# Neighbourhood attention's first keys and queries: other places in the pool, and loads ahead of the fill's third W block

## The chip, the core and the metric

The kernel runs on one core of a Trainium2 chip. The metric is the device time of one execution in microseconds, as the median of the runs. PE is TensorE (matmuls; PEld its weight loads), ACT is ScalarE, DVE is VectorE, POOL is GpSimd, and SP is SyncE, which here does nothing but issue DMAs. L72 is line 72 of the kernel.

## What is computed

One layer of an encoder on 1024 tokens of width 1024 in float32: a half-step SwiGLU, a mixing layer, a half-step SwiGLU. The mixing layer projects its input to queries, keys and values of a retention and of a 2-D neighbourhood attention and to gates, runs both, and merges them. The change is at the start of the neighbourhood attention:

```python
u = rms_norm(x, mix_pre_norm)
ret_q, ret_k, ret_v, ret_g, na_q, na_k, na_v, gate_ret, gate_na = split(u @ w_mix_in)
# neighbourhood attention: 8 heads of 64, tokens on a 16 x 64 grid
for each row r and block of 16 query columns:
    k, v = 8 rows x 32 columns around the block
    s = (q / 8) @ k.T + rel_bias, masked to 8 x 16 around each query
    o = softmax(s) @ v
```

## The kernel before

**Arithmetic.** Float32 products are made of reduced ones: `split` (L55 to L65) makes of a tile a high part on ACT (L61, or L64 with a scale) and a low part on DVE (L62, L65), and `mm3` (L85 to L90) sums three matmuls, high by high, high by low and low by high.

**W blocks.** `load_w` takes a 512 KB block of weights from DRAM with one DMA on SP (L72) into a tile `wraw` (4 buffers) and splits it in two pieces `wh`, `wl` (8 buffers each).

**The work before.** The projections for attention and gates run as `Pairs`, with operands a11, a12, a22 and the sums s1 to s4, high and low parts of 8 KB in a partition each. In the last of these jobs PE reads them in the order s2, a12, s3, s1, a22, s4. The pool that holds s1 to s4 is then closed, and its bytes are given to the pools `mix` and `na`.

**Neighbourhood attention** is `na_cores`. It runs over 4 pairs of heads, and for each pair over 8 units (`NA_UNITS`: which bias, which half of the rows, which column block). `load(hp)` takes the pair's keys (`kraw`, L879) and splits them into `k0` and `k1`; `qload(hp)` takes its queries in four DMAs (L867) into two tiles `qraw`; `qsplit` makes the operands `qh`, `ql` of one column block. `scores` (L909 the matmuls, L910 to L918 the softmax), `flip` (L928, transposes) and `values` are the three stages, run one unit behind each other. `load(hp + 1)` comes in unit 4 of a pair and `qload(hp + 1)` in unit 5; `qraw` has two buffers and a pair uses both, so the next pair's queries wait until `qsplit` has read the old ones for the last time (unit 4). The tile `ot` takes a pair's output, which POOL stores (L978).

**The fill.** PE's time between these stages is filled with other matmuls: `fill` is a generator `products()`, which yields after each `mm3`. Its first part is `vproj` for retention's values: 2 halves of the columns, each in groups of 3, 3 and 2 token tiles, each over 8 k-tiles, with one W block for two k-tiles. `fill(12)` is called ahead of unit 0, then 2 + 2 steps in each unit. So the third W block of the first group (k = 4) is asked for at step 12, of the second at step 36 (unit 6), and in the second half of the columns at steps 76 (unit 16) and 100 (unit 22).

**What sets the order.** The kernel names tiles; a scheduler turns the program into one fixed list for each engine. It takes instructions by their place in the program, but one whose operands or bytes aren't free yet lets later ones pass. Each engine and the SP queue then work their list strictly in order. A tile gets its bytes by the order in which a pool's tags are first asked for, and with `reuse_waits="tile"` its first use waits for the last use of just those earlier tiles that lay there. Before, the order in `na` is kraw, k0, k1, qraw, the q operands, bt, s, the v tiles, pth, ptl, ot, from byte 77152 of a partition on. Retention's pool `ret` later begins at the same byte.

After the fill's steps have run past retention's values, `ret_cores` follows; its first v tiles (L1069) lie at byte 101728.

## Time and profile before

| | |
|---|---|
| median of 3 runs | 2270.53 us (2268.02 to 2271.82) |
| the profiled execution | 2266.95 us |
| its span, first to last instruction | 2265.2 us |
| granted PE clock, mean over the span | 0.992 |
| PE busy | 2204.2 us |
| DMA | 439.91 MB, 194 GB/s |

Times in the profile are microseconds from the span's start. A row of a timeline gives start, length, engine, line, operation, what it writes and reads, how many were merged, and in brackets the engine's idle time before it with what ended it. A row SPq is a DMA's issue, not its transfer. A row of waits gives who waited for whom, the sum, how often, and the longest. Matmuls overlap: a row's 0.39 us is its own length, and the next one starts 0.23 us later. Of PE's idle time nothing comes back by itself: the span ends when PE's list ends.

### The profile page before, as it was taken

Reading aid. Unit: us, or ns where it says so; the run is one execution under the profiler, and the core shown is the slowest. Engines: PE = TensorE matmul, PEld = TensorE weight load, DVE = VectorE, ACT = ScalarE, POOL = GpSimd, SP = SyncE. Lnnn points to the kernel's source line nnn. Section 1 sums busy time; section 2 is a strip of 40 time slices with the busy share of each in tenths; the row PEclk is TensorE's granted clock in tenths of the full one; section 3 lists DMA queues with packets and bytes.
Section 4 is the critical chain, followed back from the end, with each engine's and each line's share of the span. In section 5 each row is a group of like instructions: output and inputs, shape, how many; then the busy total and the mean of one; then the engine's idle time right before and its main releaser. Section 6 shows DMA issues by size and latency. Waiting matters only on the chain. (4 is left out here: it accounts for less than half of the span.)

```text
span 2265.2 us, 30039 instructions
## 1 busy us (share of the span) xinstructions
PE 2204.2 (97%) x10232; PEld 1830.1 (81%) x10232; DVE 1641.4 (72%) x2928; ACT 984.5 (43%) x2054; POOL 575.8 (25%) x747
## 2 busy tenths in 40 slices
PE   6899999999998999999999999999999999999998
PEld 5688888888786887878888888887778888888886
DVE  7898878765558757769885678544998787876444
ACT  5444434332344322248885676323644343433232
POOL 1121212168521122311101222101112121215942
PEclk9999999999999999999999999999999999999999
DMA  6354434597545554557655466764345444449765
GB/s 251 134 181 150 177 130 170 187 387 294 199 174 174 180 173 134 145 181 241 217 173 174 151 230 233 259 232 144 117 156 188 149 161 147 154 157 378 283 225 180
DMA packets 150345, 439.91 MB, mean 194 GB/s; under 512 B 19056, under 2 KB 46832, under 8 KB 148080
## 3 DMA queue, kind: packets, MB, share of 16 engines
q1 hardware_dynamic: 108912, 305.84, 39.4%
q0 software_dynamic: 41280, 132.15, 16.2%
q8 instruction: 81, 1.33, 0.2%
q14 instruction: 72, 0.59, 0.1%
HBM read 297.41 MB, written 144.70 MB: 195 GB/s over the span
## 5 line engine op out<-in xcount | busy, mean ns | idle before, releaser
L62 DVE TENSOR_TENSOR wl<-wraw,wh 128x512 fp32r<-128x512 f32 x472 | 317.1, 689 | 66.3 <-ACT wh L61 66.0
L61 ACT CAST wh<-wraw 128x512 fp32r<-128x512 f32 x476 | 274.2, 618 | 169.2 <-PE ps L89 69.2
L88 PE MATMUL ps<-wh,g 128*128 128x512 f32 x484 | 188.8, 390 | 0.0
L89 PE MATMUL ps<-wl,g 128*128 128x512 f32 x484 | 188.7, 390 | 0.0
L90 PE MATMUL ps<-wh,g 128*128 128x512 f32 x484 | 188.5, 390 | 0.0
L552 ACT ACTIVATE c<-c 128x512 f32<-128x512 f32 x88 | 55.5, 632 | 208.0 <-DVE c L517 107.6
L62 DVE TENSOR_TENSOR wl<-w,wh 128x512 fp32r<-128x512 f32 x77 | 77.9, 1031 | 86.3 <-ACT wh L61 86.1
L62 DVE TENSOR_TENSOR wl<-x,wh 128x512 fp32r<-128x512 f32 x77 | 78.4, 1035 | 78.3 <-ACT wh L61 77.1
L61 ACT CAST wh<-t 128x512 fp32r<-128x512 f32 x58 | 36.0, 621 | 195.0 <-DVE t L511 194.9
L88 PE MATMUL ps<-a11h,wh 128*128 128x512 f32 x276 | 111.5, 404 | 7.9 <-ACT wh L61 7.9
L90 PE MATMUL ps<-a11h,wl 128*128 128x512 f32 x276 | 109.7, 398 | 7.3 <-DVE wl L62 7.2
L90 PE MATMUL ps<-a12h,wl 128*128 128x512 f32 x276 | 108.7, 394 | 3.4 <-DVE wl L62 3.4
L88 PE MATMUL ps<-a12h,wh 128*128 128x512 f32 x276 | 109.7, 397 | 0.5 <-ACT wh L61 0.3
L89 PE MATMUL ps<-a11l,wh 128*128 128x512 f32 x276 | 109.8, 398 | 0.1
L90 PE MATMUL ps<-a22h,wl 128*128 128x512 f32 x280 | 109.3, 390 | 0.6 <-DVE wl L62 0.6
L88 PE MATMUL ps<-a22h,wh 128*128 128x512 f32 x280 | 109.8, 392 | 0.0
L89 PE MATMUL ps<-a22l,wh 128*128 128x512 f32 x280 | 109.2, 390 | 0.0
L89 PE MATMUL ps<-a12l,wh 128*128 128x512 f32 x276 | 108.2, 392 | 0.0
L89 PEld LDWEIGHTS ps<-wl,g 128*128 128x128 f32 x484 | 90.9, 188 | 19.1 <-DVE wl L62 0.5
L90 PEld LDWEIGHTS ps<-wh,g 128*128 128x128 f32 x484 | 90.9, 188 | 18.8
L88 PEld LDWEIGHTS ps<-wh,g 128*128 128x128 f32 x484 | 90.9, 188 | 18.7
L88 PE MATMUL ps<-s2h,wh 128*128 128x512 f32 x232 | 91.9, 396 | 6.6 <-ACT wh L61 6.5
(438 smaller groups left out, 6411.4 us busy)
## 6 DMA issues: line engine op xcount, KB each, us to landing
wraw<-in_dram SPq DMA_DIRECT2D x202, 512.0 KB, 4.5
g<-g0s SPq DMA_DIRECT2D x44, 512.0 KB, 4.2
g<-g1s SPq DMA_DIRECT2D x44, 512.0 KB, 4.9
g<-g0a SPq DMA_DIRECT2D x33, 512.0 KB, 3.3
g<-g1a SPq DMA_DIRECT2D x33, 512.0 KB, 4.5
g0s<-gth POOLq DMA_DIRECT2D x44, 256.0 KB, 4.7
g0s<-cmb POOLq DMA_DIRECT2D x44, 256.0 KB, 3.7
g1s<-gth POOLq DMA_DIRECT2D x44, 256.0 KB, 4.6
```

The costliest lines, as they stand in the source:

```text
L61: self.done = [nc.scalar.copy(h, src).ins, (eng or nc.vector).tensor_tensor(l, src, hf, ALU.subtract).ins]
L62: (eng or nc.vector).tensor_tensor(l, src, hf, ALU.subtract).ins]
L88: mm(ps, a[0], b[0], start=start, stop=False)
L89: mm(ps, a[0], b[1], start=False, stop=False)
L90: mm(ps, a[1], b[0], start=False, stop=stop)
L552: nc.scalar.activation(gate[j], gate[j], AF.Silu)
```

## The change

- `na_cores` asks for the queries first: `qload(0)` stands ahead of `load(0)`, and `k0`, `ot`, `k1` get their places in this order. The pool's order is then qraw, kraw, k0, ot, k1, the q operands and the rest.
- The names of all loads of keys and queries of `na_cores` go into a list `qk`. When `vproj` asks for a W block at k = 4 or 6 and the list isn't empty, the DMA of that block gets an edge of order to all of them (no semaphore: they are on the same queue), and the list is emptied. It is filled again by the loads of the next pairs.

```diff
     def raw(self, src, n=D):
-        self.nc.sync.dma_start(raw[:, :n], src)
+        self.fetch = self.nc.sync.dma_start(raw[:, :n], src).ins
         return raw
+
+    def after(self, e, names):
+        for n in names:
+            self.tc.add_manual_dep(e, n, mybir.DependencyInfo(
+                mybir.DependencyClass.NoSync, mybir.DependencyReason.DATA), reason="order")
...
-def na_cores(c, pool, d, bias, fill, n0, n1, n2, side={}):
+def na_cores(c, pool, d, bias, fill, n0, n1, n2, side={}, first=None):
+    first = [] if first is None else first
     def qload(hp):
...
-                nc.sync.dma_start(qraw[hp][e][64 * half:64 * half + 64], d["nq"][hp][64 * e:64 * e + 64])
+                e_ = nc.sync.dma_start(qraw[hp][e][64 * half:64 * half + 64], d["nq"][hp][64 * e:64 * e + 64])
+                first.append(e_.ins.name)
     def load(hp):
         kr = pool.tile([P, S], F32, tag="kraw", name="kraw", bufs=1)
-        nc.sync.dma_start(kr, d["nk"][hp])
-
-        kop[hp] = [pool.tile([P, S], F32R, tag=f"k{e}", name=f"k{e}", bufs=2) for e in range(2)]
+        first.append(nc.sync.dma_start(kr, d["nk"][hp]).ins.name)
+
+        kop[hp] = []
+        for e in range(2):
+            kop[hp].append(pool.tile([P, S], F32R, tag=f"k{e}", name=f"k{e}", bufs=2))
+            if e == 0 and not ots:
+                ots[0] = pool.tile([P, 16, 64], F32, tag="ot", name="ot", bufs=2)
...
+    qload(0)
     load(0)
-    qload(0)
     qsplit(0, 0)
     fill(n0)
...
+    qk = []
     def vproj(src, groups, done):
...
                 if k % 2 == 0:
                     w = ahead.pop(k // 2) if k // 2 in ahead else c.load_w(src[k // 2])
+                    if k > 3 and qk:
+                        c.after(c.fetch, qk)
+                        qk.clear()
...
-        na_cores(c, na, d, bias, fill, *NA_FILL, {12: lambda: dec.append(Decays(c, mix, logits, dtab))})
+        na_cores(c, na, d, bias, fill, *NA_FILL, {12: lambda: dec.append(Decays(c, mix, logits, dtab))}, qk)
```

## The prediction

> **What bounds the kernel now.** I read the page first, then the waits of PE around the start of neighbourhood attention, then the timelines of PE, SP and ACT there, then the DMA and windows views. The page:

> ```profile
> span 2265.2 us, 30039 instructions
> ...
> PE 2204.2 (97%) x10232; PEld 1830.1 (81%) x10232; DVE 1641.4 (72%) x2928; ACT 984.5 (43%) x2054; POOL 575.8 (25%) x747
> ```

> PE is the bound: 2265.2 - 2204.2 = 61.0 us of idle in the whole span is all that a change of order can win, apart from time in which PE runs at a lower clock. The waits of PE from 1003 to 1043 us (what waited, for what, sum, times, longest):

> ```profile
> PE ps L909 <- ACT qh L64: 3.2, 1, 3.2
> PE ps L88 <- ACT pth L61: 1.1, 2, 0.6
> PE pt L928 <- DVE s L918: 0.8, 2, 0.6
> PE pt L928 <- DVE ptl L62: 0.4, 1, 0.4
> ```

> One wait stands out: the first score matmul (L909) waits 3.2 us for the split of q. The three rows below it sum to 2.3 us and belong to the first softmax units. PE's timeline shows where it lies:

> ```profile
> 1011.52 0.39 PE L88 MATMUL ps<-wh,a12h 128*128 128x512 f32 x1
> ...
> 1014.46 0.39 PE L89 MATMUL ps<-wl,a12h 128*128 128x512 f32 x1
> 1018.07 0.45 PE L909 MATMUL ps<-k,qh 128*128 128x384 f32 x1 [3.21 <-ACT qh L64]
> ```

> The fill's twelve steps end at 1011.52 (there its operand changes to a12, the fill's third W block). From there the scores could run; PE takes 14 more fill matmuls, is then idle for 3.21 us, and after it pays in clock. The windows view (length, busy time of PE, PEld, DVE, ACT, POOL, then the granted clock, DMA share, GB/s):

> ```profile
> 1015.00:1018.00 3.00, 0.00 (x0) 0.00 (x0) 2.94 (x5) 2.95 (x7) 0.00 (x0) 1.00 1.00 285
> 1018.00:1024.00 6.00, 5.93 (x20) 4.93 (x21) 5.14 (x22) 2.42 (x9) 0.00 (x0) 0.72 0.40 141
> ...
> 1027.00:1043.00 16.00, 13.69 (x82) 10.97 (x82) 14.96 (x43) 14.93 (x39) 3.69 (x4) 1.00 0.82 294
> 1043.00:1060.00 17.00, 17.00 (x101) 15.16 (x101) 16.77 (x48) 14.55 (x42) 1.41 (x1) 1.00 0.74 225
> ```

> In the six us after the wait the clock is 0.72: 6 x 0.28 = 1.7 us lost. From 1043 PE is full again. Why q and k are late stands in the timelines of SP and ACT and the DMA view:

> ```profile
> 985.84 14.53 SPq L72 DMA_DIRECT2D wraw<-in_dram  x5
> ...
> 1006.37 0.42 SPq L879 DMA_DIRECT2D kraw<-nk  x1
> 1006.89 2.45 SPq L867 DMA_DIRECT2D qraw<-nq  x4
> ```

> ```profile
> 1014.24 2.30 ACT L61 CAST k<-kraw 64x512 fp32r<-64x512 f32 x4 [3.89 <-DMA kraw<-nk]
> ...
> 1017.60 0.72 ACT L64 ACTIVATE qh<-qraw 128x256 fp32r<-128x256 f32 x2
> ```

> ```profile
> kraw<-nk SPq DMA_DIRECT2D x1, 512.0 KB, 7.8
> qraw<-nq SPq DMA_DIRECT2D x4, 256.0 KB, 9.0
> ```

> Five W blocks leave SP from 985.84 on (the fill's third to seventh), an eighth later, and only at 1006.37 the load of k. It lands 7.8 us later, at 1014.2; ACT has stood idle for it 3.89 us, casts k for 2.30, then two W pieces, then q.

> **The change, part by part.** It adds no instruction of an engine and no DMA; it moves five loads and adds edges of order.

> *Other places.* In the program's allocation the pool begins at byte 77152 of a partition, and in front of it lay the old operands s2h (71520 to 79712), s3l (to 87904), s3h (to 96096), s4l (to 104288), s2l (to 112480), s1h (to 120672), s4h. Before, k lies over s2h and s3l, but both q tiles over s4l. Now q takes 77152 to 85344 (s2h, s3l), k 85344 to 89440 (s3l, s3h), the first buffer of k0 lies over s3h, that of k1 over s2l. So the last reader that q, k and the splits of k wait for is s3h:

> ```profile
> 994.97 0.39 PE L90 MATMUL ps<-s3h,wl 128*128 128x512 f32 x1
> ```

> *Order.* The third W block may leave SP only behind these five loads. So SP sends q and k from about 995.4 on: the four q loads take 2.45 us, k 0.42, all are out by 998.3, 8.5 us before now. With the longest landings above (9.0 and 7.8 us) all have landed by 1006.8. The k casts (2.30), the first q casts (0.72) and DVE's subtractions behind them (one of 0.69, the page's L62 row below) end at about 1010.5, ahead of 1011.52. The third W block, sent at 998.3 instead of 985.84, has 13.2 us until PE needs it, against at most 9.0 to land and 1.3 to split: hidden, with 2.9 us in hand. If that cover went (q, k and four W blocks together at the rate of a full DMA row), the lateness would be paid on PE.

> Gain of this part: 3.2 (the wait) + 1.7 (the clock) = 4.9 us. The 2.3 us of the small waits are late next; DVE is busy 14.96 of 16 us there, though 3 us of splits leave that stretch, so I take no change, with -2.3 as the other end.

> *The edges that come later.* The list of loads is not only filled once: load(1) and qload(1) add to it in units 4 and 5, and the next third W block (step 36 of the fill, unit 6) then has to follow them; the same at step 100 in unit 22 with qload(3). There the q loads wait until the last split of the pair before has read its tile, so they cannot be early. SP's rows of these q loads and PE's first matmul of the W block that must now follow:

> ```profile
> 1042.34 3.38 SPq L867 DMA_DIRECT2D qraw<-nq  x4
> ```

> ```profile
> 1049.59 0.40 PE L88 MATMUL ps<-wh,a12h 128*128 128x512 f32 x1
> ```

> ```profile
> 1126.46 2.73 SPq L867 DMA_DIRECT2D qraw<-nq  x4
> ```

> ```profile
> 1134.42 0.40 PE L88 MATMUL ps<-wh,a12h 128*128 128x512 f32 x1
> ```

> What a W block costs from issue to matmul, from the page:

> ```profile
> wraw<-in_dram SPq DMA_DIRECT2D x202, 512.0 KB, 4.5
> ```

> ```profile
> L62 DVE TENSOR_TENSOR wl<-wraw,wh 128x512 fp32r<-128x512 f32 x472 | 317.1, 689 | 66.3 <-ACT wh L61 66.0
> L61 ACT CAST wh<-wraw 128x512 fp32r<-128x512 f32 x476 | 274.2, 618 | 169.2 <-PE ps L89 69.2
> ```

> So 4.5 + 0.62 + 0.69 = 5.8 us. Issue of the first: 1042.34 + 3.38 + 0.1 = 1045.8; ready 1051.6; needed 1049.59: 2.0 us late. The second: 1129.3 + 5.8 = 1135.1 against 1134.42: 0.7 late. In the program before these blocks were fetched tens of us ahead, so this wait is new, and no row shows it. Bounds: 0 if PE's order puts softmax work in front of that step (the scores, transposes and value matmuls of a unit need no W block), and with the 9.0 us of a crowded queue instead of 4.5, 6.5 and 5.2 us. A gain is excluded, since the block only comes later. I take 2.0 + 0.7 = 2.7, since the 4.5 us is the median of 202 such loads. Behind the waiting fill matmul on PE stand the transposes and values of the unit before.

> *The tile ot.* It now lies at 97632 to 105824, and its second buffer, which pair 3 uses, under the first v tiles of retention (101728). These must wait for the last store of ot. The rows of POOL, of that tile's landings (min, median, max), of SP's v loads and of PE's first matmul with v:

> ```profile
> 1193.62 0.54 POOL L68 DMA_DIRECT2D no<-ot  x1
> ```

> ```profile
> DMA to landing us min/median/max: 4.2/6.6/9.0
> ```

> ```profile
> 1193.07 1.48 SPq L1069 DMA_DIRECT2D vraw<-rv  x3
> ```

> ```profile
> 1205.16 0.36 PE L88 MATMUL ps<-vh,kdh 128*128 128x256 f32 x1
> ```

> With the median landing the loads leave at 1200.2; with the shortest load of this stretch's kind (about 3 us, estimated from the 4.5 of a block of twice the size) and the split they are ready at 1204: no cost. With 9.0 it is 1206.6: 1.5 us. Below zero is excluded: the wait is new. I take 0.

> *Sum*: -4.9 + 2.7 + 0 = -2.2 us. Against the profiled execution (2266.95 us, span 2265.2 and 1.75 around it) that is 2264.75. That execution lies 3.58 us below the median of the three runs, 2270.53, so the predicted median is 2268.3.

> [...] The rows show an idle stretch of 3.21 us and a clock of 0.72 in the 6 us behind it, and a clock of 1.00 from 1027 to 1043 beside waits of 0.6 us at most. [...]

> **Rivals.**

> *The new waits are hidden* (chance 0.2). The start is won and PE's order has softmax work where the W block is late. For it: a unit's own work is independent of the fill. Against it: PE takes its queue in order, and the order is set ahead. Time: 2270.5 - 4.9 = 2265.6, with the 2.3 us of small waits 2263.3.

> *The late W blocks cost more than the start gains: slower* (0.2). The place is steps 36 and 100, the mechanism SP's queue: the block stands behind 1 MB of q. The price at the upper bounds is 6.5 + 5.2 = 11.7 us, and twice the 1.7 us of clock that the one wait of over 3 us in these rows cost, 15.1 in all: 2270.5 - 4.9 + 15.1 = 2280.7. It decides from a common lateness of 4.9 us on, that is, landings of about 5.6 us instead of 4.5 (twice 1.1 more). For it: 9.0 us was the landing of q loads in this very kernel. Against: in these two stretches the loads stand among less traffic than at 1006. The middle of this case is 2275.

> *The change doesn't do what it says* (0.1): q and k leave SP at 995, but their splits stand on ACT and DVE behind work that itself comes late, or the W blocks now crowd them in the DMA queues, and the first score still comes at about 1018. Then only the small losses are left: 2270.5 to 2273.

> **How the numbers follow.** The forecast, -2.2, has 0.5; its own range is 2266 to 2271 (no late blocks' share, or twice it). What a measurement of this kernel can tell from no change is about 0.2%, 4.5 us. Faster by more than that (below 2266.0): nearly all of the first rival and a little of the forecast, 0.2. Slower by more (above 2275.1): half of the second rival with the tails of unknown order elsewhere, 0.15. The rest, 0.65. The range for 8 in 10 reaches from the hidden waits, 2263, to the middle of the slower case and a little beyond, 2277.

> **What would show it.** Right: SP's q loads at 995 to 998 ahead of the W loads; the L909 wait gone and a clock of 1.00 at 1018; PE waiting on L88 for wh or wl of a W block at the second pair's q loads and once more 85 us later; SP's v loads of retention behind the store of ot. Wrong: the first score at 1018 as before, no wait at steps 36 and 100, or a wait of PE at the third W block itself (about 1012).

## The result and the profile after

The changed kernel takes 2274.81 us (median of 11 runs, 2272.56 to 2276.75) where the kernel before takes 2269.62 us on the same chip (11 runs, 2265.70 to 2273.15). The ratio is 1.0022 with a 95% interval of 1.0014 to 1.0031: slower by 5.2 us, where 2.2 us less had been forecast. The time lies inside the range that was given, on the other side of the forecast.

The page of the profiled execution after (all lines of `kernel.py` behind line 72 have moved down: the score matmul is now L920, the transposes L939, the fill's three matmuls L93 to L95, the split L61 and L62 as before):

```profile
span 2271.3 us, 30002 instructions
...
PE 2205.5 (97%) x10232; PEld 1829.3 (81%) x10232; DVE 1645.1 (72%) x2928; ACT 983.0 (43%) x2054; POOL 578.1 (25%) x747
```

TensorE has the same 10232 matmuls and 1.3 us more of busy time; the rest of the 6.1 us of span is waiting. SP's timeline shows that the loads did what was meant (start, length, queue, line, operation, tiles, count):

```profile
992.75 2.41 SPq L873 DMA_DIRECT2D qraw<-nq  x4
995.26 0.52 SPq L886 DMA_DIRECT2D kraw<-nk  x1
1001.10 0.35 SPq L910 DMA_DIRECT2D bt<-in_dram  x1
1001.54 0.40 SPq L72 DMA_DIRECT2D wraw<-in_dram  x1
```

q and k left at 1006.89 and 1006.37 before. Measured against the same TensorE instruction (matmul 4221, below) that is 11.7 and 8.7 us earlier now, and they had landed by 999.7 and 1000.9 (k 5.6 us behind its issue, where the prediction allowed 7.8):

```profile
kraw<-nk SPq DMA_DIRECT2D x1, 512.0 KB, 5.6
```

But the waits of TensorE from 995 to 1210 us (what waited, for what, sum, times, longest) begin with a longer wait of the first score, not with none:

```profile
PE ps L920 <- DVE k L62: 6.2, 2, 5.9
PE pt L939 <- DVE s L929: 1.5, 1, 1.5
PE ps L94 <- DVE wl L62: 0.2, 1, 0.2
```

It was 3.2 us for q; it is 5.9 us for k:

```profile
1015.13 0.69 PE L920 MATMUL ps<-k,qh 128*128 128x384 f32 x1 [5.90 <-DVE k L62]
```

ScalarE's timeline says what it did with operands that had been there since 1001 (the bracket is the idle time before and what ended it):

```profile
1003.77 0.22 ACT L1003 ACTIVATE dect<-dect 128x8 f32<-128x8 f32 x1
1009.30 0.21 ACT L1034 ACTIVATE decq<-decq 128x8 f32<-128x8 f32 x1 [5.30 <-DVE decq L1026]
...
1009.64 0.70 ACT L64 ACTIVATE qh<-qraw 128x256 fp32r<-128x256 f32 x2
1012.00 0.63 ACT L1034 ACTIVATE decm<-decm 128x512 f32<-128x512 f32 x1 [1.65 <-DVE decm L1031]
1012.53 0.70 ACT L64 ACTIVATE qh<-qraw 128x256 fp32r<-128x256 f32 x2
1013.14 2.28 ACT L61 CAST k<-kraw 64x512 fp32r<-64x512 f32 x4
1015.45 1.14 ACT L61 CAST wh<-wraw 128x512 fp32r<-128x512 f32 x2
```

ScalarE stood still for 5.30 us with the split of q fourth in its list. What it waited for is `Decays`, the side job of unit 12 that prepares the retention's decay tables; the lists have it ahead of the splits. (In the kernel before, the same chain runs from 1007.83 to 1012.35, while both engines have no k yet, and its end comes behind the splits.) Its VectorE half is a chain in which each step reads the step before; VectorE's timeline has its first and last steps:

```profile
1004.02 0.18 DVE L1004 TENSOR_SCALAR dect<-dect 128x8 f32<-128x8 f32 x1 [1.92 <-ACT dect L1003]
...
1008.49 0.18 DVE L1014 SCALAR_TENSOR_TENSOR dect<-dect 128x8 f32<-128x8 f32 x1
1008.70 0.23 DVE L1026 TENSOR_SCALAR decq<-dect,dectb 128x4 f32<-128x4 f32 x1
...
1013.78 2.61 DVE L62 TENSOR_TENSOR k<-kraw,k 64x512 fp32r<-64x512 f32 x4
```

From 1004.02 to 1008.70 there is one step of 8 columns every 0.21 us. The splits of q and k stand behind it in the lists of both engines, and the casts of the third W block (1015.45) behind those of k. So TensorE has neither scores nor fill. The windows view (length, busy time of PE, PEld, DVE, ACT, POOL, then the granted clock, DMA share, GB/s) shows the price:

```profile
1003.00:1015.00 12.00, 6.23 (x28) 4.83 (x26) 9.57 (x44) 5.01 (x14) 0.30 (x1) 0.93 0.62 232
1015.00:1018.00 3.00, 2.56 (x6) 1.96 (x7) 2.94 (x9) 2.08 (x4) 0.00 (x0) 0.50 0.00 0
1018.00:1024.00 6.00, 6.00 (x26) 4.96 (x26) 4.95 (x17) 4.16 (x11) 0.00 (x0) 0.82 0.61 196
...
1027.00:1043.00 16.00, 15.86 (x94) 13.82 (x93) 15.36 (x40) 13.42 (x36) 4.21 (x5) 1.00 0.48 145
```

The clock is 0.50 and then 0.82, where before it was 0.72 for six us only. In exchange TensorE is nearly full from 1027 to 1043: 15.86 us of 16, against 13.69 before. Most of the 2.3 us of small waits there is gone; 1.5 us of waiting for the softmax comes back later, at 1109.78 (the second row of the waits above).

**How long the stages take.** Some of the difference of two profiles is scatter, so each kernel was measured between the same TensorE instructions, whose order is the same in all kernels outside 1011 to 1139 us. *Attention* below runs from matmul 4221 of TensorE's list (it starts at 1005.17 in the profile before, at 1002.72 after) to matmul 5094 (1165.15 and 1166.17): 159.98 us before, 163.46 after. *Head 4* is the last head of retention, from matmul 6032 (1330.01 and 1331.06) to 6296 (1375.21 and 1379.58): 45.20 and 48.52 us. Between the two nothing changed: 164.86 before and 164.88 after.

The gaps between TensorE's matmuls, and its time at half clock, say where the two stages lost. In the attention they are 6.4 + 1.7 us before and 8.3 + 2.3 us after; the other 0.9 us of difference is busy time of the same matmuls in another order. The start alone, the first 40 us behind matmul 4221, has 7.2 us of both before (8.8 in a second profile of that kernel) and 8.7 after: it won nothing, and lost at most 1.5 us. In head 4 they are 0.1 + 0 before and 1.6 + 1.7 after.

### The profile page after: what moved, and what is told of

It is laid out like the page before. It is cut to its first block, busy times and chain, and to the rows that moved or that the text cites. A ratio compares the mean times of both kernels' runs of the same rounds, so it can differ in the third digit from the quotient of the medians.

```text
span 2271.3 us, 30002 instructions
## 1 busy us (share of the span) xinstructions
PE 2205.5 (97%) x10232; PEld 1829.3 (81%) x10232; DVE 1645.1 (72%) x2928; ACT 983.0 (43%) x2054; POOL 578.1 (25%) x747
## 5 line engine op out<-in xcount | busy, mean ns | idle before, releaser
L62 DVE TENSOR_TENSOR wl<-wraw,wh 128x512 fp32r<-128x512 f32 x472 | 316.1, 686 | 66.5 <-ACT wh L61 66.1
L61 ACT CAST wh<-wraw 128x512 fp32r<-128x512 f32 x476 | 272.3, 618 | 157.6 <-PE ps L94 62.7
L93 PE MATMUL ps<-wh,g 128*128 128x512 f32 x484 | 188.6, 390 | 0.0
L95 PE MATMUL ps<-wh,g 128*128 128x512 f32 x484 | 188.3, 389 | 0.0
L62 DVE TENSOR_TENSOR wl<-w,wh 128x512 fp32r<-128x512 f32 x77 | 78.4, 1038 | 85.8 <-ACT wh L61 85.7
L62 DVE TENSOR_TENSOR wl<-x,wh 128x512 fp32r<-128x512 f32 x77 | 79.2, 1045 | 76.6 <-ACT wh L61 74.9
L61 ACT CAST wh<-t 128x512 fp32r<-128x512 f32 x58 | 36.0, 621 | 193.7 <-DVE t L516 193.6
L93 PE MATMUL ps<-a11h,wh 128*128 128x512 f32 x276 | 110.9, 402 | 8.2 <-ACT wh L61 8.2
L95 PE MATMUL ps<-a11h,wl 128*128 128x512 f32 x276 | 109.3, 397 | 7.4 <-DVE wl L62 7.2
L95 PE MATMUL ps<-a12h,wl 128*128 128x512 f32 x276 | 108.9, 394 | 3.4 <-DVE wl L62 3.4
L93 PE MATMUL ps<-a12h,wh 128*128 128x512 f32 x276 | 110.1, 399 | 0.5 <-ACT wh L61 0.3
L93 PE MATMUL ps<-a22h,wh 128*128 128x512 f32 x280 | 109.9, 392 | 0.0
L95 PE MATMUL ps<-a22h,wl 128*128 128x512 f32 x280 | 109.2, 390 | 0.6 <-DVE wl L62 0.6
L93 PEld LDWEIGHTS ps<-wh,g 128*128 128x128 f32 x484 | 90.9, 188 | 18.9
L95 PEld LDWEIGHTS ps<-wh,g 128*128 128x128 f32 x484 | 90.9, 188 | 18.7
L93 PE MATMUL ps<-s2h,wh 128*128 128x512 f32 x232 | 91.9, 396 | 7.7 <-ACT wh L61 7.7
## 6 DMA issues: line engine op xcount, KB each, us to landing
wraw<-in_dram SPq DMA_DIRECT2D x202, 512.0 KB, 4.6
g<-g0s SPq DMA_DIRECT2D x44, 512.0 KB, 4.7
g<-g1s SPq DMA_DIRECT2D x44, 512.0 KB, 4.7
g<-g0a SPq DMA_DIRECT2D x33, 512.0 KB, 3.4
g<-g1a SPq DMA_DIRECT2D x33, 512.0 KB, 4.7
g0s<-gth POOLq DMA_DIRECT2D x44, 256.0 KB, 4.8
g0s<-cmb POOLq DMA_DIRECT2D x44, 256.0 KB, 3.7
g1s<-gth POOLq DMA_DIRECT2D x44, 256.0 KB, 4.6
```

Source lines behind the costliest of these rows:

```text
L61: self.done = [nc.scalar.copy(h, src).ins, (eng or nc.vector).tensor_tensor(l, src, hf, ALU.subtract).ins]
L62: (eng or nc.vector).tensor_tensor(l, src, hf, ALU.subtract).ins]
L93: mm(ps, a[0], b[0], start=start, stop=False)
L95: mm(ps, a[1], b[0], start=False, stop=stop)
```

## The experiments

Theory 1, formed on these rows: early q and k are of no use because `Decays` stands in front of their splits in the lists of ScalarE and VectorE. Theory 2: the W blocks that now follow q loads cost the time. Theory 3: the new places cost it, or what lies behind the attention does. "Decays late" is a kernel whose `Decays` is put behind the first splits by two edges of order, without a semaphore. All runs in one table (us; the difference is that of the medians of the kernel and of the kernel before in the same batch; "wait" is TensorE's wait at the first score in the profile, in brackets if it falls in pieces):

| kernel | median | difference | ratio, 95% interval | wait | attention | head 4 |
|---|---|---|---|---|---|---|
| before | 2269.62 | | | 3.21 | 159.98 | 45.20 |
| before, second profile | 2271.5 (one run) | | | 3.74 | 161.52 | 46.23 |
| changed | 2274.81 | +5.2 | 1.0014 to 1.0031 | 5.90 | 163.46 | 48.52 |
| changed, second profile | 2276.6 (one run) | | | 5.88 | 164.22 | 47.85 |
| Decays late | 2266.15 | -3.8 | 0.9979 to 0.9996 | none | 156.00 | 47.19 |
| places alone | 2273.33 | +3.4 | 1.0008 to 1.0029 | 2.04 | 162.22 | 47.81 |
| first order alone | 2270.65 | +0.7 | 0.9999 to 1.0016 | 5.89 | 161.34 | 46.73 |
| before, Decays late | 2270.45 | +0.5 | 0.9999 to 1.0020 | 2.79 | 162.93 | 46.56 |
| first order, Decays late | 2264.99 | -4.3 | 0.9972 to 0.9991 | none | 155.22 | 45.79 |
| no order, Decays late | 2271.59 | +2.4 | 1.0003 to 1.0025 | 0.48 | 161.11 | 46.50 |
| first order, Decays late, ot at the end | 2263.34 | -5.9 | 0.9962 to 0.9983 | none | 154.77 | 45.80 |
| orders in the kernel before | 2275.22 | +6.0 | 1.0018 to 1.0039 | (5.79) | 164.46 | 46.86 |
| changed, ot at the end | 2273.72 | +3.4 | 1.0014 to 1.0031 | 5.90 | 163.32 | 48.28 |
| Decays late, ot at the end | 2266.41 | -3.9 | 0.9972 to 0.9991 | none | 155.02 | 47.58 |

The two right columns account for most of the third. Against the mean of the two profiles before (160.75 and 45.72) they sum to +5.5 for the changed kernel (measured +5.2), -3.3 for Decays late (-3.8), -5.9 for the fastest (-5.9), +4.9 for the orders in the kernel before (+6.0). Ten of the eleven changed kernels come within 1.8 us this way; "before, Decays late" misses by 2.5. Each profile is one execution, and the two of the kernel before differ by 1.5 and 1.0 us in these columns, so no single value is good to better than about that. For the changed kernel, 2.7 of the 5.5 us lie in the attention and 2.8 in head 4.

**Decays late.**

```diff
     c.split(kop[hp][e][es, bs], kop[hp][e][es_, bs], kr[es, bs], eng=nc.gpsimd if hp and b else None)
+    if not hp:
+        c.ksplit = c.done
...
-        nc.vector.tensor_scalar(a, x, -1.0, None, ALU.mult)
+        e1 = nc.vector.tensor_scalar(a, x, -1.0, None, ALU.mult)
...
-        nc.scalar.activation(e, a, AF.Exp)
+        e2 = nc.scalar.activation(e, a, AF.Exp)
+        c.after(e1.ins, [c.ksplit[1].name])
+        c.after(e2.ins, [c.ksplit[0].name])
```

> The changed kernel with one addition: the first VectorE and the first ScalarE instruction of Decays are put behind the last split of the first keys in their engines' lists. Theory 1 (the lists: the serial chain of Decays, 38 small steps, stands in front of the first splits of q and k, so that early q and k are of no use): the first split of q leaves at about 1001 (q lands at 999.7) and not 1009.6, that of k by about 1005, TensorE's 5.9 us wait at the first score and the clock of 0.50 and 0.82 behind it are gone, and the time falls by 7 to 9 us against the changed kernel, to 2266 to 2268, below the kernel before by 1 to 4. Theory 2 (W blocks held behind q loads): the W orders are all still there, so the time stays within 2 us of the changed kernel's 2274.8. Theory 3 (the places, or the stretch behind the attention): as theory 2, with the 3.4 us at the retention's last head and 1.7 us at 1560 to 1705 still there.

Measured 2266.15 us, 3.8 below the kernel before and, by the differences of the table, 9.0 below the changed kernel. ScalarE's timeline of this kernel:

```profile
1001.60 1.32 ACT L64 ACTIVATE qh<-qraw 128x256 fp32r<-128x256 f32 x4
1002.83 2.28 ACT L61 CAST k<-kraw 64x512 fp32r<-64x512 f32 x4
1005.29 1.14 ACT L61 CAST wh<-wraw 128x512 fp32r<-128x512 f32 x2 [0.18 <-DMA wraw<-in_dram]
```

and its TensorE at the same place:

```profile
1008.07 0.39 PE L95 MATMUL ps<-wh,a11l 128*128 128x512 f32 x1
1008.30 0.34 PE L922 MATMUL ps<-k,qh 128*128 128x384 f32 x1
...
1010.08 0.50 PE L94 MATMUL ps<-wl,a12h 128*128 128x512 f32 x1 [0.44 <-DVE wl L62]
```

The splits run as soon as their data is there, and the first score follows the last fill matmul of the twelve steps without a gap. The third W block, which left SP at 1000.77, costs 0.44 us. The windows view has the clock at full speed:

```profile
1008.00:1015.00 7.00, 6.47 (x30) 4.94 (x28) 5.00 (x18) 4.35 (x10) 0.00 (x0) 1.00 0.64 227
1015.00:1018.00 3.00, 2.96 (x17) 2.60 (x18) 3.00 (x10) 3.00 (x9) 0.00 (x0) 1.00 1.00 314
1018.00:1024.00 6.00, 6.00 (x36) 5.31 (x35) 5.88 (x18) 5.96 (x15) 2.01 (x3) 1.00 0.27 107
```

Theory 1 holds for the start: the loads, places and orders are those of the change, and moving the chain alone takes the wait away.

**Decays late in the kernel before.** The same edit in the kernel before.

> The kernel before with the same addition as in the first of these runs: Decays behind the first keys' splits. Theory 1: its q lands only at about 1014, behind most of Decays, so the chain's place matters little there: 2268 to 2271, the wait at the first score 2.5 to 3.5 us. If Decays late is by itself worth 7 us or more (2263 or less), or costs 3 us or more because it now falls among the softmax steps (2272 or more), then the first of these runs cannot be read as theory 1 reads it.

Measured 2270.45 us, the wait 2.79 us: no difference that can be told. There k lands only 8.6 us behind matmul 4221 (1011.31 - 1002.69) and q after it, and what stands in front of their splits hardly matters. So the chain has a price only together with early loads, and early loads have a worth only without the chain in front.

**Places alone.** The orders are left out:

```diff
-                    if k > 3 and qk:
-                        c.after(c.fetch, qk)
-                        qk.clear()
```

> The changed kernel without the orders between the q and k loads and the W blocks; the new places stay. Theory 1: Decays still stands ahead of the splits of q and k in VectorE's list, but the third W block is split before them and gives TensorE fill work; the wait at the first score is between 1 and 4 us (before: 3.2, changed kernel: 5.9), the time 2268 to 2272. Theory 2: with the orders gone the loss is gone: 2265 to 2269, and no wait at the steps of the second and third pair. Theory 3 (the places cost): 2274 to 2276 as the changed kernel.

Measured 2273.33 us: no theory's time. SP's timeline of this kernel:

```profile
1005.55 0.33 SPq L72 DMA_DIRECT2D wraw<-in_dram  x1
...
1006.98 2.42 SPq L873 DMA_DIRECT2D qraw<-nq  x4
1009.51 0.52 SPq L886 DMA_DIRECT2D kraw<-nk  x1
```

Without the order a W block that waits for a free buffer until 1005.55 stands in front of q, so q is hardly earlier than before (0.6 us against matmul 4221), and k, now behind q, leaves 2.5 us later. The first score starts 16.2 us behind matmul 4221, not 12.9 as before; the W block that is split ahead of it leaves a wait of only 2.04 us there, but a transpose waits another 1.84 us for the softmax at 1028.74, and the clock falls twice, for 3.2 us of loss instead of 1.7. So the places and the exchange of q and k give nothing by themselves, and the median is 3.4 us worse, 2.1 of which the profile has in head 4. The order for the third W block is what makes q early.

**The first order alone.** Only the third W block gets its order; the lists of the later pairs are ignored.

```diff
-    qk = []
+    qk, firsts = [], []
...
-                    if k > 3 and qk:
+                    if k > 3 and len(qk) > 4 and not firsts:
                         c.after(c.fetch, qk)
-                        qk.clear()
+                        firsts.append(k)
```

> The changed kernel with the order kept for the third W block alone; the W blocks near the second and third pairs' q loads are free again. Theory 1: the start is as in the changed kernel (wait 5.9 us, clock 0.5), so the time is 2273 to 2276. Theory 2 as it was predicted blind (2.0 and 0.7 us at steps 36 and 100): 2272. Theory 2 in its dear form (most of the 5.2 us of loss comes from there): 2269 to 2271. Theory 3: 2274 to 2276.

Measured 2270.65 us with the same wait of 5.89 us at the start: 4.2 below the changed kernel (4.5 by the differences of the table). Theory 1 expected 2273 to 2276 and missed; the time is that of theory 2 in its dear form. But the W blocks themselves are not late in the changed kernel. Its TensorE timeline at step 36 and SP's rows of the same block:

```profile
1049.19 0.50 PE L93 MATMUL ps<-wh,a12h 128*128 128x512 f32 x1
1050.36 0.50 PE L94 MATMUL ps<-wl,a12h 128*128 128x512 f32 x1 [0.19 <-DVE wl L62]
```

```profile
1039.83 2.79 SPq L873 DMA_DIRECT2D qraw<-nq  x4
1042.66 0.58 SPq L72 DMA_DIRECT2D wraw<-in_dram  x1
```

0.19 us in place of the 2.0 that were predicted; at step 100 the same wait is 0.06 us (predicted: 0.7). Of the 4.2 us the profiles show 2.1 to 2.9 in the attention, of which 0.8 is a wait of a transpose for the softmax (the row of 1.5 us in the waits of the changed kernel, at 1109.78; 0.7 us here at 1105.84) and about 1 us is TensorE's busy time in another order, and 1.1 to 1.8 in head 4. With Decays late the same step is worth 0.5 us (from -3.8 to -4.3) or 2.0 (from -3.9 to -5.9) by the differences of the table, with intervals that overlap. That the later orders cost something with the chain in front is likely; how much, by which of the moved splits, and whether anything is left of it without the chain, stays open.

**Both edits, and the rest of the square.** Decays late and the first order alone; the same with the first `ot` at the end of the pool, as in the kernel before; and all orders with `ot` at the end. The edit of `ot`:

```diff
-            if e == 0 and not ots:
-                ots[0] = pool.tile([P, 16, 64], F32, tag="ot", name="ot", bufs=2)
```

> Two edits together: Decays behind the first splits, and the order kept for the third W block alone. Theory 1 (the lists at the start) and a separate loss of the orders at the second and third pair (2274.8 to 2270.65 in the run with the first order alone, 1.6 to 2.1 us of it seen in the profiles between steps 12 and 24): both gains add up, to 2262 to 2265. If the later orders cost nothing of themselves and the 4.2 us were scatter: 2266, as with Decays late and all orders.

> As the first of these runs, with the first ot allocated at the end of the pool as in the kernel before (k1, bt and the tiles behind them move down by 8 KB). Theory 1: ot's place is no part of the start, the same time as the first within 1.5 us, the wait at the first score stays away. Theory 3 (places): bt's place is free earlier or later and moves the third W block, which stands behind bt on SP at 1001; then a wait of 1 to 3 us at the third W block or at the first additions of bt, and 2 us more or less.

> Decays late, ot at the end of the pool, all orders of the change: the fourth of a square (all orders or the first alone; ot early or at the end: 2266.15, 2264.99, 2263.34 so far, with Decays late in all). If the later orders and ot's place each cost their 1.2 and 1.65 us: 2264.5. If the later orders cost the 4.2 us that they cost with Decays in front: 2267 or more.

Measured 2264.99, 2263.34 and 2266.41 us. The gains add up in small part at most. The place of `ot` makes no difference that these intervals tell apart in either row of the square (2266.15 and 2266.41; 2264.99 and 2263.34). The version with 2263.34 us beats the kernel before by 0.27% (interval 0.17% to 0.38%). The largest wait that is left there is that of a fill matmul for ScalarE's copies to `ot`, 1.44 us at 1057.51.

**No order, Decays late.**

> Decays late, the new places, none of the orders. In the run with the places alone the third W block waited on SP for a free place until 1005.55, and q left behind it at 1006.98, not at 992.75. Theory 1: early q needs the first order; without it q leaves at about 1007, the wait at the first score stays at 2 to 3.5 us and the time at 2268 to 2271. If the places alone were enough once Decays is out of the way: 2262 to 2266.

Measured 2271.59 us. q leaves at 1005.17, as in the run with the places alone. The first score waits for 0.48 us only, since here the third W block is split ahead of q and TensorE has fill work, but the wait returns one step later:

```profile
PE pt L941 <- DVE s L931: 3.4, 1, 3.4
PE pt L941 <- DVE ptl L62: 2.2, 3, 1.3
PE ps L922 <- DVE k L62: 0.7, 2, 0.5
```

TensorE's idle time over the attention is 6.6 us, between the 6.4 and 7.9 us of the two profiles before: data is as late as there, and fill only decides which instruction stands at the end of the wait. The time came out a little above the 2268 to 2271 that theory 1 expected; the place of the wait was missed.

**The orders in the kernel before**, with its places and k ahead of q.

> The orders of the change in the kernel before: its places and its k ahead of q, Decays where the lists put it. Theory 1: k's old place (under SP's wait until 1005) keeps q at 1006 whatever is behind it, so the orders only make the third W block late: a wait of 3 to 6 us at the first score and little fill for it, 2270 to 2275. Theory 3 (the new places are what costs in the change): no loss here, 2268 to 2270.

Measured 2275.22 us, as slow as the changed kernel, with none of the new places. k leaves at 994.72 and q at 1002.88, earlier than expected, but Decays stands between the casts of k and those of q, and the third W block leaves at 1006.02:

```profile
PE ps L916 <- ACT qh L64: 2.6, 1, 2.6
PE ps L916 <- DVE ql L65: 2.0, 1, 2.0
...
PE ps L916 <- DVE k L62: 1.2, 1, 1.2
```

The new places are not needed for the loss of the changed kernel: it is there without them, and in the next run it stays when one of them is taken back. That they cost nothing in other company is not shown (the run with the places alone, +3.4 us); with early q and k and a late chain they do no harm (-3.8 to -5.9).

**The change with `ot` at the end of the pool.**

> The changed kernel with the first ot at the end of the pool again; Decays stays in front of the splits, all orders stay. bt and with it the third W block leave SP at about 995.5 instead of 1001.1. Theory 1 (the Decays chain in front of the splits of q and k and of the third W block): the early bt and W block change nothing, the first score still waits 5 to 6 us, 2273 to 2276. Theory 3 (the wait is there because ot's place makes bt and the third W block late): the W block bridges the wait, which falls to 1 to 3 us, 2267 to 2271.

Measured 2273.72 us. SP's timeline, then the waits:

```profile
998.16 0.37 SPq L908 DMA_DIRECT2D bt<-in_dram  x1
998.62 0.38 SPq L72 DMA_DIRECT2D wraw<-in_dram  x1
```

```profile
PE ps L918 <- DVE k L62: 6.2, 2, 5.9
```

In this profile q leaves at 995.01, 2.3 us later than in the profile after, so the third W block left 5.2 us earlier measured against q. The wait is the same to the hundredth. An early W block does not bridge it, since its casts stand behind the chain as well.

**A second profile of each kernel.**

> The kernel before once more, for a second profile of it. If what the changed kernel's profile lost behind the attention, at 1330 to 1375 (3.1 us) and 1600 to 1705 (1.7 us), is scatter between executions, this profile has 31 to 33 and 106 to 109 us there, and not 30.2 and 105.1 again. If it has 30.2 and 105.1 again, the change or every edit of it costs something there (all seven experiments so far showed 30.8 to 32.8 and 106.8 to 109.0).

> The changed kernel once more, for a second profile of it. Theory 1: the wait at the first score is 5.9 us again, since the lists set it; the attention from the same instruction on takes 163 to 164 us (163.46 in the first profile, 159.98 and 161.52 in the two of the kernel before). GpSimd's 35th pow took 1.74 us in the changed kernel and in eight experiments, 0.56 us in both profiles of the kernel before and in the two fastest experiments: if that belongs to the program it is 1.74 again, if it is chance between executions it can be 0.56, and the retention's last head then takes 30.5 to 31.5 us instead of 33.25.

The first profile of the kernel before lies at the lower end: its second has 161.52 and 46.23 us in the two stages, and 108.05 where the first had 105.11 between the matmuls at 1600 and 1705 us. So what the changed kernel lost in that last stretch (106.81) lies within scatter, and so does about 1 us of its loss in head 4. The changed kernel's second profile has the wait of 5.88 us again, 164.22 in the attention, and the slow pow of the last section again; the part of head 4 behind its first 15.03 us takes 32.82 us, near the 33.25 of the first and not 30.5 to 31.5.

## Why the prediction was wrong

- **The failing step is the end of the splits.** The prediction took the landing of q and k, added 2.30 + 0.72 + 0.69 us for the splits, and had them "end at about 1010.5, ahead of 1011.52". The loads were no obstacle (both had landed at 1000.9 instead of the 1006.8 that was allowed for), and the casts took the 2.3 and 0.7 us of the sum. What it left out is the position in the lists of two engines: ScalarE stood for 5.30 us before a `Decays` step (1009.30) with q in memory and its split behind that step in the list. The splits of k ended at 1016.4 (1013.78 + 2.61).
- **The term of -4.9 us was not earned at the start**, which came out even or up to 1.5 us worse (8.7 us of idle time and lost clock against 8.8 and 7.2). With the chain out of the way it is earned: the same sum is 1.1 us in "Decays late", and attention is 4.8 us shorter than the mean of the profiles before (156.00 against 160.75), with the orders all in place. That 4.8 and 4.9 agree so well is partly luck, since small waits that the prediction left alone went too and 1.1 us of busy time came in addition.
- **The third rival had the mechanism and too low a price.** "Their splits stand on ACT and DVE behind work that itself comes late" was given 0.1 and 2270.5 to 2273. It counted only the small losses. In the kernel before 14 fill matmuls (14 x 0.23 = 3.2 us) shorten the wait; in the changed one the W block that they need is split behind k, so the wait grows from 3.21 to 5.90 although the first score starts 0.5 us earlier against matmul 4221. And the clock behind it costs 0.50 x 2.9 + 0.18 x 6 = 2.5 us (2.3 without the small waits in it), not 1.7.
- **The new waits at steps 36 and 100**, +2.7 us, are 0.2 us: that term was wrong, and the rival in which they are hidden was right on it, for its reason: TensorE's list has other work in front, and step 36 comes 46.5 us behind matmul 4221 (1049.19 - 1002.72) instead of 44.4 (1049.59 - 1005.17). With Decays late, where the start is won, the waits for W blocks sum to 1.1 us, 0.44 of it at the third block. In exchange, the later orders seem to cost up to 4.5 us in other places while the chain stands in front, which the prediction named only as "unknown order elsewhere".
- **The third W block** was to be hidden with 2.9 us in hand. As to its load that is so: with Decays late it costs 0.44 us.
- **The small waits of 2.3 us** were left unchanged; about 2.2 of them went (13.69 to 15.86 us of 16).
- **`ot` under the retention's v tiles**, 0: right; the 164.86 us behind the attention are 164.88.
- **What lay outside the prediction** is 1.6 to 3.3 us in head 4, by which of the two profiles of each kernel are compared; the last section has what is known of it. Without it the changed kernel would still not be faster.
- **Two small sums.** All five loads were to be out by 998.3; that is 11.0 us ahead of the end of the old q loads (1006.89 + 2.45), not 8.5. And the upper bound for `ot` adds up to 1206.4 (1202.6 and the same 3.8 us as in the median case), not 1206.6. Neither changes a term.

## What to carry to other kernels

Here data that arrived early was used early only where its consumer was next in its engine's list: q landed at 999.7 and was split at 1009.64 behind `Decays`, and in "Decays late" at 1001.60. For other kernels that is a thing to look for: ahead of a moved load, read the lists of the engines that consume it, and look for a serial chain of small steps in front of it, such as one that stands in an idle stretch which the move is about to remove. An order edge for the load may need its counterpart for the work that now competes with the split. And a wait is priced with the fill that stood in it: here the fill that moved out of the wait of 3.21 us left one of 5.90.

## What the runs showed of the hardware

```profile
1013.46:1016.87 3.41, 1.70 (x7) 1.18 (x8) 3.34 (x8) 1.93 (x5) 0.00 (x0) 1.00 1.05 332
1016.87:1020.28 3.41, 3.41 (x10) 2.65 (x9) 1.70 (x7) 2.73 (x5) 0.00 (x0) 0.50 0.62 245
```

TensorE is idle for 1.71 us of the first stretch, and the second is at half clock: 0.50 x 3.41 = 1.7 us, the same as behind the 3.21 us of the kernel before. The two first profiles have seven falls in that part. Each follows a stretch in which TensorE was idle for 1.60 to 3.41 us in sum; the longest sums without a fall behind them are 1.60 us (before, from 684.59) and 1.59 us (after, from 613.94). So in these profiles about half a stretch was enough, and where a wait lies on the grid matters (a wait of 1.60 us that the grid cuts left the clock at 1.00, below). In the changed kernel the wait of 5.90 us fills the stretch from 1009.89 to 1013.30, and its end and a wait of 0.32 us take 2.1 us of the next: the clock is at half for two stretches, 6.83 us. The prediction priced waits of 2.0 us at their own length, which nothing in its rows showed (they have no wait of TensorE between 0.6 and 3.2 us); by these falls such a wait could have cost 1.7 us more, an estimate.

**One pow that takes 1.74 us.** GpSimd's 35th pow of the program (`rstd`, 128x1) takes 0.56 us or 1.74 us, and always the same in the two profiles of one kernel. GpSimd's timelines of the changed kernel and of the kernel before:

```profile
1345.11 1.74 POOL L103 TENSOR_TENSOR rstd<-ss,mhalf 128x1 f32<-128x1 f32 x1 [6.85 <-DVE ss L1135]
```

```profile
1342.38 0.56 POOL L98 TENSOR_TENSOR rstd<-ss,mhalf 128x1 f32<-128x1 f32 x1 [6.85 <-DVE ss L1124]
```

It is 1.74 or 1.73 us in the changed kernel and in eight experiments, 0.56 us in the kernel before and in the two fastest experiments. In the changed kernel TensorE waits 1.58 us behind it, at 1350.69, and the clock falls. The windows view on the grid of the clock, for its first profile and then for its second:

```profile
1347.81:1351.22 3.41, 1.81 (x12) 1.31 (x11) 3.09 (x8) 3.09 (x8) 0.59 (x1) 1.00 0.95 339
1351.22:1354.64 3.42, 3.42 (x14) 3.03 (x14) 2.48 (x9) 2.15 (x8) 0.56 (x1) 0.50 0.52 161
```

```profile
1348.45:1351.86 3.41, 1.89 (x10) 1.16 (x9) 2.68 (x7) 3.41 (x10) 0.59 (x1) 1.00 0.96 358
1351.86:1355.27 3.41, 3.32 (x20) 2.99 (x21) 2.48 (x9) 1.82 (x7) 0.56 (x1) 1.00 0.54 173
```

In the first profile 1.58 us of wait and 1.7 us of clock make the 3.3 us by which head 4 is longer than in the first profile of the kernel before, in a place that no edit touches. In the second the pow takes 1.74 us and TensorE waits 1.60 us again, but the grid cuts that wait, 1.52 us of idle time lie in one stretch, and the clock stays at 1.00; of the other kernels with the long pow, "changed, ot at the end" shows the fall too (a clock of 0.89 from 1350 to 1365, as in the first profile of the changed kernel), while "Decays late", "first order alone" and "Decays late, ot at the end" have 1.00 there. The idle time ahead of the pow is the same 6.85 us in the changed kernel and the kernel before, and the instructions around it have the same order. What decides between the two durations was not found.
